# Two feed-forwards of a two-block float32 kernel: gate and up as two-by-two block products with seven multiplications, down as a second phase

## The chip, the core and the metric

The kernel runs on one core of a Trainium2 chip. The metric is device time in microseconds, from the start to the end of one execution; three executions of the kernel before gave 3000.35 us in the median (3000.02 to 3003.03). The profile is taken from one further execution. Its engines are TensorE (matrix products), VectorE, ScalarE and GpSimd (elementwise work) and SyncE, whose queue issues the DMAs.

## What is computed

Two transformer blocks of different kinds follow each other, all in float32, on 1024 tokens of width 1024. Each has two kinds of attention, an output projection, a gated feed-forward of width 2816, and a gated layer embedding ("ple"). Only the feed-forwards change:

```python
# block 1, after h = h + rmsnorm(mix, attn_post_norm[i])
u = rmsnorm(h, ffn_pre_norm[i])
gate, up = jnp.split(u @ w_gate_up[i], [D_FF], axis=-1)      # (1024, 1024) @ (1024, 2 * 2816)
y = (jax.nn.silu(gate) * up) @ w_down[i]                     # (1024, 2816) @ (2816, 1024)
h = h + rmsnorm(y, ffn_post_norm[i])
h = h + (p[i] @ ple_proj[i]) * jax.nn.sigmoid(h @ ple_gate[i])

# block 2
def conv_ffn(h, w_gate, w_up, conv_w, conv_b, w_down):       # called with rms_norm(x, ffn_norm_g[i])
    s = h.shape[1]
    g = h @ w_gate
    gp = jnp.pad(g, ((0, 0), (CONV_WIDTH - 1, 0), (0, 0)))   # CONV_WIDTH = 3, along the tokens
    conv = conv_b
    for j in range(CONV_WIDTH):
        conv = conv + gp[:, j:j + s, :] * conv_w[j]
    return (jax.nn.silu(conv) * (h @ w_up)) @ w_down
```

## The kernel before

TensorE multiplies float32 as three products of split numbers. `split` makes of a tile a high part (a cast on ScalarE to a 32-bit type that the array takes, line 135) and a low part (a subtraction, line 141, on VectorE or GpSimd). `mm3` (lines 210 to 212) issues high x high, high x low and low x high into one PSUM bank. Every matmul has 128 rows, 128 columns of weights and 512 streamed columns.

The stages follow each other in time: attention of block 1, its output projection (`out1`), feed-forward `ffn(0)` from 700 to 1428 us, `ple1`, attention of block 2, `out2` to 2162 us, `ffn(1)` to about 2880, `ple2`. In `out1` and `out2` each tile of 128 tokens gets its product with the output weights, a norm, the residual (GpSimd, line 932), another norm (`u_tok`, line 453); then `transpose_split` turns it on TensorE with eight transposes and splits it into `u[half]`, the operand of the feed-forward with features on the partitions; `half` is four token tiles.

`ffn` goes over pairs of the 22 blocks of 128 hidden features. `gu_mm(f, half)` multiplies a block of gate and of up with half of the tokens, 24 matmuls each; ScalarE applies the activation (in block 2 VectorE first convolves), VectorE multiplies gate and up, and the result is split into `act`, which stays in SBUF. After a pair's four calls, `down` multiplies both blocks of `act` with their rows of `w_down` for all eight token tiles, 96 matmuls, and adds the result to `y` from PSUM.

```python
for f0, n in CHUNKS:            # pairs of blocks
    for f, h in order:
        gu_mm(f, h)             # gate and up of one block, 512 tokens: 2 x 24 matmuls
    for i in range(NT):
        down(f0, n, i)          # 2 halves of the width x 2 blocks x 3 matmuls
```

The order of the work is the order in which the program is written; each engine takes its instructions in that order and waits for what it needs. Weights come through the class `Weights`: a list of units of 512 KB in the order of use, loaded by SP into two raw buffers and split into slots (four for kind "w", gate and up; three for kind "x", down) as `pump`, called after every step, finds a free slot.

Of the kernel before, what the change touches and what calls it, by code (L numbers as in the profile page):

```python
# [8 lines left out]
F32 = mybir.dt.float32  # L9
F32R = mybir.dt.float32r  # L10
# [36 lines left out]
CHUNKS = [(f, 2) for f in range(0, NF, 2)]  # L47


class Weights:  # L50
# [3 lines left out]
    def __init__(self, k, raws):  # L54
        self.k, self.raws = k, raws
        self.src, self.kind, self.tile, self.raw = [], [], {}, {}
# [4 lines left out]
    def open(self, kind, slots, ctx):  # L61
        self.pool[kind] = self.k.pool(kind + str(self.n_split), slots, ctx=ctx)
        self.slots[kind] = slots
        self.live[kind] = 0

    def add(self, src, kind="w"):
        self.src.append(src)
        self.kind.append(kind)
        return len(self.src) - 1

    def _dma(self):
        u = self.n_dma
        raw = self.k.rawp.tile([P, 1024], F32, tag="raw", name="raw")
        a, b = self.src[u].shape[1:]
        self.k.nc.sync.dma_start(out=raw.rearrange("p (a b) -> p a b", a=a) if b * a == 1024 else
                                 raw.rearrange("p (a b) -> p a b", a=a)[:, :, 0:b], in_=self.src[u])
        self.raw[u] = (raw, a, b)
        self.n_dma += 1

    def _split(self):  # L80
        k, u = self.k, self.n_split
        while self.n_dma <= u:
            self._dma()
        raw, a, b = self.raw.pop(u)
        kind = self.kind[u]
        w = self.pool[kind].tile([P, 2, 1024], F32R, tag=kind, name=kind)
        view = lambda t: t.rearrange("p (a b) -> p a b", a=a)[:, :, 0:b]
        k.split(view(w[:, 0, :]), view(w[:, 1, :]), view(raw), k.w_hi, k.w_lo[u % len(k.w_lo)])
# [3 lines left out]
        while self.n_dma < len(self.src) and self.n_dma - self.n_split < self.raws:  # L92
            self._dma()
# [6 lines left out]
    def pump(self, n=9):  # L100

        while n and self.n_split < len(self.src):
            kind = self.kind[self.n_split]
            if self.live[kind] >= self.slots[kind]:
                break
# [8 lines left out]
class Kernel:  # L114
# [119 lines left out]


# [29 lines left out]
    def row_units(self, name, r0, n):  # L265
        w = self.A[name][0]
        return [self.W.add(w[(r0 + j) * P:(r0 + j + 1) * P, :].rearrange("p (a n) -> p a n", a=1), "x") for j in range(n)]
# [30 lines left out]
    def ffn_units(self, s, gate, up, u0, down):  # L298
        U = self.U
        for f0, n in CHUNKS:  # L300
            for f in range(f0, f0 + n):
                U["g", s, f] = self.a_units(gate, f * P, 1)[0]
                U["u", s, f] = self.a_units(up, u0 + f * P, 1)[0]
            for f in range(f0, f0 + n):
                U["d", s, f] = self.row_units(down, f, 1)[0]
# [44 lines left out]
    def build(self):  # L350
# [4 lines left out]
        self.rawp = self.pool("raw", RAWS)  # L355
        self.W = Weights(self, RAWS)
        self.W.open("w", 4, self.ctx)
# [5 lines left out]
            rm=[4, 2, T], dv=[T, 512], omT=[512, T], od=[T, 512], bias8=[4, 1152], skew=[4, P * 1152]).items()}  # L363
# [92 lines left out]
    def block1(self):  # L456
# [9 lines left out]
        with ExitStack() as c1:  # L466
            self.up = self.pool("u_a", 2, ctx=c1)
            with ExitStack() as c2:
                yp = self.pool("y", 1, ctx=c2)
                self.y = [yp.tile([P, D], F32, tag=f"y{i}", name=f"y{i}") for i in range(NT)]  # L470
                self.W.open("x", 3, c2)
                self.out1()
                self.pre = self.pool("pre0", 1, ctx=c2)

                nc.sync.dma_start(out=S["skew"].rearrange("h (r x) -> h r x", r=P),
                                  in_=S["bias8"].unsqueeze(1).to_broadcast([4, P, 1152]))
                self.ffn(0)
                self.ple1()
            rest = self.block2_in(c1)
            self.mla(rest)  # L480
        with ExitStack() as c1:
# [1159 lines left out]
```

## Time and profile before

| | us |
|---|---|
| median of three runs | 3000.35 |
| profiled execution, whole | 3009.19 |
| profiled execution, span from first to last instruction | 3007.4 |
| TensorE busy | 2888.8 (96% of the span) |
| VectorE, ScalarE, GpSimd busy | 1559.0, 1030.8, 398.2 |
| `ffn(0)`; `ffn(1)` | from 700 to 1428; from 2162 to about 2880 |

Times from the trace are counted from the span's start. "Busy" of TensorE counts a matmul from its start to the end of its last column, and matmuls overlap; the rate is read from the distance between two starts. A bracket at the end of a timeline row gives how long the engine was idle before it and what it waited for.

### The profile page before, as it was taken

What the parts mean: (1) busy time and instruction counts of PE and PEld (TensorE: products, weight loads), DVE (VectorE), ACT (ScalarE), POOL (GpSimd) and SP (SyncE); (2) the same over time, 40 slices, a digit from 0 to 9 for tenths busy, and PEclk for the clock granted to TensorE, in tenths of its full rate; (3) what the DMA queues carried; (4) which work ended last, traced back from release to release, by engine and by line L of the source; (5) the groups of instructions that cost most, each with busy time, mean ns of one, the idle gap of its engine ahead of it and who ended that gap; (6) DMA issues with size and microseconds to landing.
All of it is one profiled execution on the core that took longest, in us unless ns stands there. A gap on an engine that the chain in (4) does not pass through costs nothing.

```text
span 3007.4 us, 36884 instructions
## 1 busy us (share of the span) xinstructions
PE 2888.8 (96%) x14227; PEld 2384.4 (79%) x14227; DVE 1559.0 (52%) x3004; ACT 1030.8 (34%) x2096; POOL 398.2 (13%) x444
## 2 busy tenths in 40 slices
PE   8989998889999999999899999989999999999999
PEld 6878776777888888888788788767888888888877
DVE  4444678754233232334568775778744444444462
ACT  4121566643211111112236455656421211122231
POOL 1223000131100010011314100010011111111111
PEclk9999999999999999999999999989999999999999
DMA  4112554334211111111135764864311111111111
GB/s 132 64 50 99 147 146 124 130 130 128 63 42 50 42 51 48 49 57 56 55 113 159 204 162 129 192 170 104 102 54 45 49 57 42 50 43 56 42 65 46
DMA packets 256622, 266.80 MB, mean 89 GB/s; under 512 B 12278, under 2 KB 204826, under 8 KB 254910
## 3 DMA queue, kind: packets, MB, share of 16 engines
q1 hardware_dynamic: 256446, 264.44, 30.1%
q8 instruction: 112, 1.84, 0.3%
q14 instruction: 64, 0.52, 0.1%
HBM read 201.43 MB, written 65.33 MB: 89 GB/s over the span
## 4 chain that ended last, share of the span: by engine, by line
PE 66%; DVE 5%; DMA 4%; ACT 1%; POOL 1%; issue 1%; SPq 0%; DVEq 0%; ACTq 0%; POOLq 0%
PE bank L212 20%; PE bank L210 20%; PE bank L211 20%; PE bank L198 1%; PE bank L1455 1%; PE bank L745 1%; DMA om_r<-rm 1%; DMA qk<-qkT 1%; DMA strip<-skew 1%; POOL y L932 1%; PE bank L758 1%; DMA o_sb<-osbT 0%; DVE qk L1207 0%; DVE y L453 0%; PE bank L1338 0%
## 5 line engine op out<-in xcount | busy, mean ns | idle before, releaser
L210 PE MATMUL bank<-u,w 128*128 128x512 f32 x1664 | 652.5, 392 | 2.3 <-DVE hq L540 1.7
L212 PE MATMUL bank<-u,w 128*128 128x512 f32 x1664 | 649.9, 391 | 0.0
L211 PE MATMUL bank<-u,w 128*128 128x512 f32 x1664 | 649.8, 390 | 0.0
L210 PEld LDWEIGHTS bank<-u,w 128*128 128x128 f32 x1664 | 312.9, 188 | 66.5 <-DVE hq L540 1.9
L212 PEld LDWEIGHTS bank<-u,w 128*128 128x128 f32 x1664 | 312.9, 188 | 64.0
L211 PEld LDWEIGHTS bank<-u,w 128*128 128x128 f32 x1664 | 312.8, 188 | 62.6
L210 PE MATMUL bank<-w,u 128*128 128x512 f32 (+1 forms) x736 | 297.8, 405 | 5.7 <-ACT w L135 3.4
L211 PE MATMUL bank<-w,u 128*128 128x512 f32 (+1 forms) x736 | 291.1, 396 | 2.2 <-POOL w L141 1.3
L212 PE MATMUL bank<-w,u 128*128 128x512 f32 (+1 forms) x736 | 292.4, 398 | 0.0
L141 DVE TENSOR_TENSOR w<-raw,w 128x1024 fp32r<-128x1024 f32 (+1 forms) x154 | 190.1, 1236 | 182.8 <-ACT w L135 182.4
L212 PE MATMUL bank<-x,act 128*128 128x512 f32 x704 | 273.9, 389 | 0.0
L210 PE MATMUL bank<-x,act 128*128 128x512 f32 x704 | 273.9, 389 | 0.0
L211 PE MATMUL bank<-x,act 128*128 128x512 f32 x704 | 273.9, 389 | 0.0
L141 POOL TENSOR_TENSOR act<-sg,act 128x512 fp32r<-128x512 f32 x88 | 136.6, 1553 | 918.3 <-ACT act L135 918.3
L994 DVE TENSOR_TENSOR sg<-sg,bank 128x512 f32<-128x512 f32 x88 | 60.5, 688 | 338.7 <-PE bank L212 336.3
L135 ACT CAST w<-raw 128x1024 fp32r<-128x1024 f32 (+1 forms) x158 | 165.1, 1046 | 138.0 <-PE bank L212 115.2
L135 ACT CAST x<-raw 128x1024 fp32r<-128x1024 f32 x53 | 55.7, 1051 | 357.2 <-PE bank L212 352.5
L210 PEld LDWEIGHTS bank<-w,u 128*128 128x128 f32 x736 | 140.2, 191 | 31.1 <-ACT u L203 4.2
L211 PEld LDWEIGHTS bank<-w,u 128*128 128x128 f32 x736 | 140.1, 190 | 27.2 <-POOL w L141 2.2
L212 PEld LDWEIGHTS bank<-w,u 128*128 128x128 f32 x736 | 140.3, 191 | 26.8 <-DVE u L206 0.2
L1012 DVE TENSOR_TENSOR yy<-yy,bank 128x512 f32<-128x512 f32 x176 | 118.6, 684 | 79.7 <-PE bank L212 79.7
L211 PEld LDWEIGHTS bank<-x,act 128*128 128x128 f32 x704 | 132.2, 188 | 27.5
(319 smaller groups left out, 4693.1 us busy)
## 6 DMA issues: line engine op xcount, KB each, us to landing
raw<-in_w_gate_up_dram SPq DMA_DIRECT2D x44, 512.0 KB
raw<-in_w_down_dram SPq DMA_DIRECT2D x44, 512.0 KB
raw<-in_w_in_dram SPq DMA_DIRECT2D x40, 512.0 KB
qk<-qkT SPq DMA_DIRECT2D x32, 384.0 KB
raw<-in_w_gate_dram SPq DMA_DIRECT2D x22, 512.0 KB
raw<-in_w_up_dram SPq DMA_DIRECT2D x22, 512.0 KB
k<-sk SPq DMA_DIRECT2D x16, 512.0 KB
raw<-in_w_out_dram SPq DMA_DIRECT2D x16, 512.0 KB
```

What stands on the lines that cost most here:

```text
L135: nc.scalar.copy(hi, src)
L141: e.tensor_tensor(lo, src, hi.bitcast(F32), ALU.subtract)
L198: nc.tensor.transpose(ps[:, j * P:(j + 1) * P], src[:, (g + j) * P:(g + j + 1) * P], self.ident)
L210: mm(ps, lh, rh, start=start, stop=False)
L211: mm(ps, lh, rl, start=False, stop=False)
L212: mm(ps, ll, rh, start=False, stop=stop)
L745: nc.tensor.transpose(ps[:, n * P:(n + 1) * P], a[:, j * P:(j + 1) * P], self.ident)
L758: nc.tensor.matmul(pv[:, 0:256], vs[:, j0, :], at[:, hl, 0:256], start=jp == 0 and hl == 0, stop=False)
L932: nc.gpsimd.tensor_tensor(y, y, x, ALU.add)
L994: nc.vector.tensor_tensor(sg, sg, pu, ALU.mult)
L1012: nc.vector.tensor_tensor(y, y, ps, ALU.add)
L1455: nc.tensor.matmul(pv[:, 0:P], at[:, n * P:(n + 1) * P], x["v"][:, j, :], start=j == 0, stop=j == i)
```

## The change

The product of the weights (a pair of blocks x 1024 features) with the tokens is taken as a two-by-two block product: the pair's two blocks are the rows, the lower and the upper 512 features the inner index, and the even and the odd token tiles the columns. It is formed with seven products of half the inner length instead of eight, from sums and differences of the four weight blocks and of the four operand blocks. A **chain** is one pair of gate or of up; there are 22 in a feed-forward. A product is 12 matmuls (4 steps of 128 features, 3 each), numbered 1 to 7. Products 1, 6, 7 and 4 go into one bank one upon the other, 5 and 3 into a second, 2 into a third, and ScalarE copies intermediate states to SBUF (`keep`), where VectorE adds them to others.

The weights of a chain are four units: the raw first block, `s12`, a difference, and a half-width one; GpSimd forms the last three with four operations on half tiles (`add_pair`). The operand blocks other than 1 and 2 are formed by `right_operands` on GpSimd and VectorE. The activated result goes to a DRAM tensor `act`, and after all chains `down` loads it back and does the 1056 matmuls that it did before. In the second feed-forward the residual also goes to DRAM (`h3`) and is loaded back as `y` ahead of `down`. Weights of `down` take slots of kind "w".

```diff
+PART = {1: (0, 0), 2: (0, 1), 6: (1, 0), 5: (1, 1), 7: (2, 0), 4: (2, 1), 3: (3, 0)}
+def sevens(s, chains):
+    if s == 0:
+        seq = [(c, p) for p in (1, 2, 6, 5, 7, 4, 3) for c in (0, 1)]
+        late = []
+    else:
+        seq = [(0, 1), (0, 2), (1, 1), (0, 6), (0, 5), (0, 7), (0, 4), (0, 3), (1, 2), (1, 6), (1, 5), (1, 7)]
+        late = [(1, 4), (1, 3)]
+    for c in range(2, chains):
+        seq += [(c, 1)] + late + [(c, 2), (c, 6), (c, 5), (c, 7)]
+        late = [(c, 4), (c, 3)]
+    return seq + late
...
+    def add_pair(self, src1, src2):
...
+        def m1(w, lo):
+            both(w, st["r1"], lo)
+        def m2(w, lo):
+            r1, r2 = st["r1"], st["r2"]
+            x = k.xp.tile([P, 1024], F32, tag="x", name="s12")
+            pool(x[:, HI], r2[:, LO], r2[:, HI], ALU.add)
+            pool(x[:, LO], x[:, HI], r1[:, LO], ALU.subtract)
+            pool(r2[:, LO], r1[:, LO], r2[:, LO], ALU.subtract)
+            pool(r1[:, HI], r1[:, HI], x[:, LO], ALU.subtract)
+            both(w, x, lo)
...
+        with ExitStack() as c1:
+            self.up = self.pool("u_b", 1, ctx=c1, side="right")
+            self.open_y(c1, 1)
+            for i in range(NT):
+                ld(out=self.y[i], in_=S["h3"][i * P:(i + 1) * P, :])
+            self.down(1)
+            self.ple2(c1)
...
-                return lambda: self.transpose_split(u, self.u[i // 4], 0, i % 4, 8)
+                return lambda: self.put_uT(u, i)
...
+    def right_operands(self, q2):
+        B11, B12, B21, B22 = (self.uT[n] for n in ((0, 0), (0, 1), (1, 0), (1, 1)))
+        T2 = self.q(q2)
+        for n, pools, value, steps in (
+                (6, (q2, q2), T2, [sub(pool, B11, B12, B11), sub(dve, T2, B22, B11)]),
+                (5, (q2, q2), B11, []),
+                (7, (q2, q2), B12, [sub(pool, B12, B22, B12)]),
+                (4, (self.q1, self.q1), B21, [sub(pool, B21, B21, T2)]),
+                (3, (q2, self.q1), B22, [])):
+            hi, lo = self.ub[n] = tuple(self.q(p, F32R) for p in pools)
+            for h in range(2):
+                c = slice(h * 256, (h + 1) * 256)
+                for f in steps:
+                    f(c)
+                self.split(hi[:, :, c], lo[:, :, c], value[:, :, c], "act", "dve")
...
+        def product(c, n):
...
+            for k in range(4):
+                nc.tensor.matmul(ps, w[:, 0, o], uh[:, k, :], start=first_mm, stop=False, skip_group_check=True)
+                nc.tensor.matmul(ps, w[:, 0, o], ul[:, k, :], start=False, stop=False, skip_group_check=True)
+                nc.tensor.matmul(ps, w[:, 1, o], uh[:, k, :], start=False, stop=k == 3, skip_group_check=True)
...
+            if n == 1:
+                keep(c, 1, ps)
+            elif n == 2:
+                ev(c, 0, 0, ps, x.pop(1))
+            elif n == 6:
+                keep(c, 2, ps)
+            elif n == 7:
+                keep(c, 3, ps)
+                ev(c, 1, 1, x["b"], x.pop(3))
+            elif n == 4:
+                ev(c, 1, 0, ps, None)
+            elif n == 3:
+                ev(c, 0, 1, ps, x.pop(2))
+            self.W.pump()
...
+            def load(f):
+                r = rp.tile([P, T], F32, tag="r", name="act_raw")
+                nc.sync.dma_start(out=r, in_=S["act"][f * P:(f + 1) * P, :])
+                a = acts[f] = actp.tile([P, 2, T], F32R, tag="act", name="act")
+                self.split(a[:, 0], a[:, 1], r, "act", "dve" if f < 2 else "gps")
...
+            for f in range(2):
+                load(f)
             for f0, n in CHUNKS:
...
                 for i in range(NT):
-                    down(f0, n, i)
+                    if i in (1, 4):
+                        load(f0 + n + i // 4)
+                    out(f0, n, i)
```

Three places show what stands in the queues. GpSimd between the residual of the last token tile and the first activated tile of `ffn(0)`, before:

```order
L932 TENSOR_TENSOR y5_5005<-y5_5005,x_res_5836 128x1024
L932 TENSOR_TENSOR y6_5006<-y6_5006,x_res_5944 128x1024
L932 TENSOR_TENSOR y7_5007<-y7_5007,x_res_6075 128x1024
L141 TENSOR_TENSOR act_6198<-sg_6199,act_6198 128x512
L141 TENSOR_TENSOR act_6254<-sg_6255,act_6254 128x512
L141 TENSOR_TENSOR act_6198<-sg_6310,act_6198 128x512
```

and after (`q` are operand blocks, `s12` and `raw` weights of a chain):

```order
L1044 TENSOR_TENSOR y_5995<-y_5995,x_res_6070 128x1024
L1101 TENSOR_TENSOR q_5006<-q_5008,q_5006 128x4x256
L1101 TENSOR_TENSOR q_5008<-q_5009,q_5008 128x4x256
L141 TENSOR_TENSOR s12_6152<-raw2_6149 128x512
L1101 TENSOR_TENSOR q_5007<-q_5007,q_6169 128x4x256
L142 TENSOR_TENSOR s12_6152<-s12_6152,raw_5172 128x512
L143 TENSOR_TENSOR raw2_6149<-raw_5172,raw2_6149 128x512
L144 TENSOR_TENSOR raw_5172<-raw_5172,s12_6152 128x512
```

Behind the last residual, where the first low part of an activation stood, are now three differences of operand blocks and the four weight operations of the first chain, one of which comes ahead of the third difference.

SP's queue at the end of gate and up of the second feed-forward, before (the last weights of down, then those of the embedding step):

```order
L75 DMA raw_22620<-in_w_down_2_dram 128x1024
L75 DMA raw_22625<-in_w_down_2_dram 128x1024
L75 DMA raw_22630<-in_w_ple_gate_2_dram 128x2x512
L75 DMA raw_22763<-in_w_ple_gate_2_dram 128x2x512
L75 DMA raw_22895<-in_w_ple_gate_2_dram 128x2x512
L75 DMA raw_22900<-in_w_ple_gate_2_dram 128x2x512
```

and after (`o` is activated output on its way to `act`, `y` the residual, `act_raw` the activations for `down`):

```order
L111 DMA raw_21878<-in_w_down_2_dram 128x1024
L592 DMA y0_21912<-h3_84 128x1024
L1181 DMA act_85<-o_21892 128x512
L111 DMA raw_21899<-in_w_down_2_dram 128x1024
L592 DMA y1_21913<-h3_84 128x1024
L592 DMA y2_21914<-h3_84 128x1024
L592 DMA y3_21915<-h3_84 128x1024
L592 DMA y4_21916<-h3_84 128x1024
L592 DMA y5_21917<-h3_84 128x1024
L592 DMA y6_21918<-h3_84 128x1024
L592 DMA y7_21919<-h3_84 128x1024
L1230 DMA act_raw_21940<-act_85 128x1024
L1230 DMA act_raw_21945<-act_85 128x1024
```

The two activation loads stand behind the store of the last output, two weight loads and all residual tiles.

ScalarE in the second feed-forward, one pair before (`g` is gate, `sg` the activated gate):

```order
L982 COPY g_22405<-bank1_22353 128x512
L993 ACTIVATE sg_22404<-cv_22410 128x512
L135 CAST act_22403<-sg_22404 128x512
L982 COPY g_22469<-bank5_22418 128x512
L135 CAST w_22480<-raw_22218 128x1024
L993 ACTIVATE sg_22468<-cv_22472 128x512
```

and after, around the same number of matmuls (`s` are the copies by `keep`, `cv` a convolved row of 1024 tokens):

```order
L219 CAST w_21501<-raw2_21374 128x1024
L219 CAST w_21524<-raw_21414 128x1024
L1167 ACTIVATE cv_21496<-cv_21496 128x1024
L219 CAST w_21544<-raw_21286 128x512
L1134 COPY s_21561<-bank1_21468 128x512
L219 CAST w_21576<-s12_21577 128x1024
L1167 ACTIVATE cv_21519<-cv_21519 128x1024
L1134 COPY s_21596<-bank1_21468 128x512
L1134 COPY s_21615<-bank0_21602 128x512
```

The second activation of `cv` now stands directly ahead of the copy of the bank that product 4 goes on to use.

## Rows read from the trace of the kernel before

**Rows 1.** The page, busy time of each engine and its share of the span
```profile
PE 2888.8 (96%) x14227; PEld 2384.4 (79%) x14227; DVE 1559.0 (52%) x3004; ACT 1030.8 (34%) x2096; POOL 398.2 (13%) x444
```

**Rows 2.** Stretches of time: start:end, length, busy us by engine, clock, DMA share, GB/s
```profile
760.00:1400.00 640.00, 640.00 (x2825) 530.11 (x2824) 195.31 (x240) 109.54 (x147) 60.11 (x39) 1.00 0.16 48
...
2162.00:2220.00 58.00, 58.00 (x264) 47.98 (x263) 33.40 (x45) 20.60 (x29) 8.57 (x11) 1.00 0.32 100
```

**Rows 3.** Timeline of TensorE, inside the first feed-forward: start us, length, instruction
```profile
899.65 0.39 PE L212 MATMUL bank<-x,act 128*128 128x512 f32 x1
...
903.96 0.39 PE L210 MATMUL bank<-x,act 128*128 128x512 f32 x1
```

**Rows 4.** Groups of instructions, 2200 to 2860: count, busy us, mean ns, idle before
```profile
L141 POOL TENSOR_TENSOR act<-sg,act 128x512 fp32r<-128x512 f32 x40 | 61.8, 1545 | 274.1 <-ACT act L135 274.1
...
L991 DVE SCALAR_TENSOR_TENSOR cv<-g,cols,cv 128x512 f32<-128x512 f32 x82 | 61.5, 750 | 2.2
...
L141 DVE TENSOR_TENSOR w<-raw,w 128x1024 fp32r<-128x1024 f32 x41 | 50.1, 1222 | 6.2 <-ACT w L135 6.2
...
L135 ACT CAST w<-raw 128x1024 fp32r<-128x1024 f32 x41 | 43.2, 1053 | 16.6 <-PE bank L212 16.6
...
L982 ACT COPY g<-bank 128x512 f32<-128x512 f32 x41 | 24.1, 589 | 175.8 <-PE bank L212 175.8
...
L989 DVE TENSOR_SCALAR cv<-g,cols 128x512 f32<-128x512 f32 x41 | 22.4, 546 | 195.0 <-ACT g L982 195.0
```

**Rows 5.** Timeline of VectorE, a low part beside work of GpSimd
```profile
952.55 1.72 DVE L141 TENSOR_TENSOR x<-raw,x 128x1024 fp32r<-128x1024 f32 x1
```

**Rows 6.** Timeline of GpSimd, alone and beside that low part
```profile
940.33 1.29 POOL L141 TENSOR_TENSOR act<-sg,act 128x512 fp32r<-128x512 f32 x1 [8.91 <-ACT act L135]
...
951.37 1.81 POOL L141 TENSOR_TENSOR act<-sg,act 128x512 fp32r<-128x512 f32 x1 [9.75 <-ACT act L135]
```

**Rows 7.** Timeline of TensorE, start of the first feed-forward
```profile
703.14 0.39 PE L211 MATMUL bank<-u,w 128*128 128x512 f32 x1
...
707.51 1.11 PE L198 MATMUL bank<-ident,u_tok 128*128 128x128 f32 x4 [3.98 <-DVE u L206]
...
720.08 1.07 PE L198 MATMUL bank<-ident,u_tok 128*128 128x128 f32 x8 [1.52 <-DVE u_tok L453]
...
720.90 0.48 PE L210 MATMUL bank<-u,w 128*128 128x512 f32 x1
```

**Rows 8.** Timeline of ScalarE, the same place
```profile
704.55 1.04 ACT L135 CAST w<-raw 128x1024 fp32r<-128x1024 f32 x1 [3.73 <-DMA raw<-in_w_gate_up_dram]
```

**Rows 9.** Timeline of GpSimd, operations on 1024 elements per partition
```profile
681.60 2.39 POOL L932 TENSOR_TENSOR y<-y,x_res 128x1024 f32<-128x1024 f32 x1 [3.78 <-DVE y L453]
...
712.97 3.31 POOL L932 TENSOR_TENSOR y<-y,x_res 128x1024 f32<-128x1024 f32 x1 [14.84 <-DVE y L453]
```

**Rows 10.** Timeline of TensorE after an idle stretch
```profile
594.69 0.63 PE L211 MATMUL bank<-w,u 128*128 128x512 f32 x1
...
597.24 0.63 PE L211 MATMUL bank<-w,u 128*128 128x512 f32 x1
```

**Rows 11.** Timeline of TensorE, start of the second feed-forward
```profile
2161.61 1.03 PE L198 MATMUL bank<-ident,u_tok 128*128 128x128 f32 x8
...
2167.37 1.06 PE L198 MATMUL bank<-ident,u_tok 128*128 128x128 f32 x8
```

**Rows 12.** Stretches of time, one weight load of 512 KB
```profile
882.00:886.00 4.00, 4.00 (x19) 3.34 (x18) 1.16 (x2) 1.56 (x3) 0.00 (x0) 1.00 0.39 131
```

**Rows 13.** Stretches of time in which the DMA engines were full
```profile
704.00:705.00 1.00, 0.00 (x0) 0.00 (x0) 0.00 (x0) 0.45 (x1) 0.00 (x0) 1.00 1.00 406
...
1900.00:1950.00 50.00, 45.50 (x279) 38.02 (x278) 36.31 (x90) 32.49 (x89) 0.00 (x0) 0.90 1.00 223
```

**Rows 14.** Timeline of TensorE, from the down projection to the embedding step
```profile
1431.72 0.50 PE L210 MATMUL bank<-x,pT 128*128 128x512 f32 x1 [2.65 <-ACT pT L203]
...
1448.80 0.69 PE L198 MATMUL bank<-ident,p_in 128*128 128x128 f32 x2 [4.94 <-DVE u L206]
```

More of the change, by code (lines that the diff above doesn't have):

```diff
@@ new lines, in _add, with _raw, load, make @@
+    def _add(self, load, make, kind):
+        self.load.append(load)
+        self.make.append(make)
+        self.kind.append(kind)
+        return len(self.kind) - 1
+    def _raw(self, where):
+        self.raw_live[where] += 1
+        return self.raw_pool[where].tile([P, 1024], F32, tag=where, name=where)
+    def add(self, src, kind="w"):
+        k, st = self.k, {}
+        a, b = src.shape[1:]
+        view = lambda t: t.rearrange("p (a b) -> p a b", a=a)[:, :, 0:b]
+        def load():
+            st["r"] = self._raw("raw")
+            k.nc.sync.dma_start(out=view(st["r"]), in_=src)
+        def make(w, lo):
+            k.split(view(w[:, 0, :]), view(w[:, 1, :]), view(st.pop("r")), k.w_hi, lo)
+            self.raw_live["raw"] -= 1
+        return self._add(("raw", load), make, kind)
@@ L80, in _split, with _loads @@
+    def _loads(self, upto):
+        while self.n_dma < min(upto, len(self.load)):
+            l = self.load[self.n_dma]
+            if l is not None:
+                if self.raw_live[l[0]] >= self.raws[l[0]]:
+                    return
+                l[1]()
+            self.n_dma += 1
     def _split(self):
         k, u = self.k, self.n_split
-        while self.n_dma <= u:
-            self._dma()
-        raw, a, b = self.raw.pop(u)
+        self._loads(u + 1)
+        assert self.n_dma > u
@@ L266, in row_units @@
         w = self.A[name][0]
-        return [self.W.add(w[(r0 + j) * P:(r0 + j + 1) * P, :].rearrange("p (a n) -> p a n", a=1), "x") for j in range(n)]
+        return [self.W.add(w[(r0 + j) * P:(r0 + j + 1) * P, :].rearrange("p (a n) -> p a n", a=1)) for j in range(n)]
     def register(self):
@@ L299, in ffn_units @@
         U = self.U
[L300 to L305, printed above, removed]
+        pairs = {}
+        for c in range(NF):
+            name, c0 = ((gate, 0), (up, u0))[c % 2]
+            w = self.A[name][0]
+            src = [w[:, c0 + (c - c % 2 + j) * P:c0 + (c - c % 2 + j + 1) * P].rearrange("(k p) n -> p k n", p=P) for j in range(2)]
+            pairs[c] = self.W.add_pair(*src)
+            U["p", s, c] = {}
+        for c, p in sevens(s, NF):
+            n = PART[p][0]
+            if n not in U["p", s, c]:
+                U["p", s, c][n] = self.W._add(*pairs[c][n], "w")
+        for f in range(NF):
+            U["d", s, f] = self.row_units(down, f, 1)[0]
     def b_steps(self, units, i_us, evac, n=512, cost=5.1):
```

297 lines of the change are left out of this document (190 added, 107 removed).

## Prediction

> **What bounds the kernel now.** First the page's busy times: TensorE is busy 96% of the span [rows 1], so a change pays only if it removes matmuls or the gaps between them. Then the busy time of each engine by stage: through the first feed-forward, and where the second one takes over from its attention block, TensorE is busy in every microsecond, at the full clock [rows 2]. Then its timeline in such a stretch: a 128x512 matmul starts every (903.96 - 899.65) / 19 = 0.2268 us [rows 3]; the 0.39 us beside each is how long one takes, not its share of the time. So inside a feed-forward time is the number of matmuls times 0.2268, and the rest is what its ends cost.
>
> **What is removed.** Gate and up of one feed-forward are 22 blocks x 2 x 2 halves x 24 = 2112 matmuls now. Afterwards they are 22 chains (a pair of blocks of gate, or of up) x 7 products x 12 = 1848; the down projection keeps its 1056. Two feed-forwards lose 2 x 264 = 528 matmuls: 528 x 0.2268 = **-119.7 us**, if TensorE stays the bound.
>
> **Does it, in the steady part?** A chain is 84 matmuls, 19.05 us; a product is 2.72 us. Per chain ScalarE makes four weight splits (3.5 tiles of 1024 columns at 1.05), three copies at 0.59 and the activations, about 8 us; VectorE the same splits' low parts (3.5 x 1.22 = 4.3) and about 3 adds, in the second feed-forward 4 us of convolution more; GpSimd four half-tile operations and some multiplications, 1.3 to 1.8 each [rows 4]: none is full. But products accumulate into one bank and ScalarE copies it between them: after product 6 the copy must be done within product 5, after product 7 within product 1 of the next chain, 2.72 us each. The queue is in order, so what stands ahead of a copy counts. The tightest place is in the second feed-forward, where ScalarE's activation of a whole convolved row stands ahead of the copy after product 7. From the end of product 4 VectorE has there: two convolutions of 1024 columns, 2 x (1.09 + 2 x 1.50) = 8.2, three low parts (1.22, 1.22, 0.61), two adds at 0.75 at most: 12.8 us, begun 0.8 us late by a copy. The activation (2 x 0.59 by the copy's row) ends at 14.8, the copy at 15.4, and it is due after six products, at 16.3. That fits by 0.9 us. What can spoil it: a low part took 1.72 us beside GpSimd's operation and GpSimd's took 1.81 beside it, 1.29 alone [rows 5, 6]. If a third of VectorE's stretch is slowed so, 12.8 grows by 1.7, a miss of 0.8; if all of it, by 5.2, a miss of 4.3. Eleven such places: 0 to 47 us. I take 0.5 each, **+5**, near the third, since GpSimd works about a third of the time. The Trainium skill (GPSIMD Engine Reference, Key points) says that GpSimd shares its SBUF interfaces with VectorE and contends with VectorE instructions that have two SBUF inputs; these rows agree, and it speaks against this change, which gives GpSimd such work in every chain.
>
> **The ends.** Before, gate and up could start on the first four token tiles while the last were normalised. Now every product streams columns of all token tiles, and only products 1 and 2 need no difference of operands. The order puts 48 matmuls ahead of the first product 6 in the first feed-forward, 36 in the second; what follows waits for GpSimd.
>
> (A) First feed-forward, in. Before, TensorE waits at 703 for tile 6 and before 720.08 for tile 7, and 48 matmuls are done at 720.90 [rows 7]. Part of that lateness was ScalarE waiting 3.73 us for a weight load [rows 8], which has long landed afterwards, so tile 7 may come up to 6 us earlier, though VectorE and ScalarE get splits of operands ahead of its norm. After tile 7's transposes come a copy (0.6), then on GpSimd two differences of 1024 elements a partition, a half-tile operation, a third difference, a half tile, then the weight's cast. The nearest rows for the wide ones are 2.39 and 3.31 [rows 9]; the half tiles 1.29 to 1.81. From the transposes' first half at 720.6: 0.6 + 3 x (2.39 to 3.31) + 2 x (1.29 to 1.55) + 1.05 = 11.4 to 14.7, so product 6 starts at 732.0 to 735.3, or 6 us earlier. Then its low part 1.22, one slow restart, and the same weight chain again for the other chain of the pair, one product behind (about 2). Against 720.90: 8 to 19 us, **+14**.
>
> A restart: after an idle stretch the matmuls started every (597.24 - 594.69) / 6 = 0.425 us [rows 10], the spacing of half the clock; some ten of them lose 2 us at most, I charge 1.
>
> (D) Second feed-forward, in. Before there is no gap [rows 2] and tile 7's transposes come at 2167.37 [rows 11]. GpSimd has four wide differences after them (9.6 to 13.2), then two half tiles (2.6 to 3.1), then the cast: from 2169.1 to 2182.3 to 2186.5. TensorE has 36 matmuls (8.2) and the transposes (1.1) from 2162.6 on. Missing: 10.4 to 14.6, a low part and a restart more: 11 to 18, **+14**.
>
> (B) First feed-forward, from gate and up to down. The activations now go through DRAM. The last stored part waits for GpSimd's multiplication, about 2.6 us after the last product (an add 0.7, a multiplication 1.3 to 1.8), and one of the two first loads back stands behind that store in SP's queue. A 512 KB load moved all its bytes within 4 us [rows 12] (131 GB/s x 4 us = 524 KB). 2.6 + 2.5 to 4 + cast 1.05 = 6 to 7.7, and a restart; 5 if the loads overlap better, 14 if the store must land first and a low part is late. **+8**.
>
> (E) Second feed-forward, the same place. SP's queue holds a weight load and seven of the eight residual tiles ahead of the two activation loads, and they can start only when the space of gate and up is free: 9 x 524 KB = 4.7 MB until the first activation has landed. In two stretches with the DMA engines full, 406 GB/s and 223 GB/s were moved [rows 13]; the first is the nearer one: weight and residual tiles of whole rows, as here. 4.7 MB / 406 = 11.6 us, / 223 = 21.2. With 2.6 before, 1 of delay, 1.05 and 1.3 for the casts: 17.5 or 27; with a restart, and up to 5 for the last activations' own wait: 15 to 33, **+20**. The Trainium skill (DMA: Bandwidth & Descriptors, Where 436 GB/s comes from) has transfers between HBM and SBUF bound by about 358 GB/s; the 406 of one microsecond is above that. By 358 the 11.6 would be 13.2.
>
> (C) From down to the layer-embedding step. Before, TensorE already waits there, 2.65 and 4.94 us [rows 14] the longest. Now its weights share four slots with down's last blocks, and the projection's load is issued behind a split that waits for them: one load (4), a cast (1.05). 24 matmuls of the gate (5.4) may go first and hide it, or not; the second embedding has the same: 0 to 10 each, **+5 twice**.
>
> **Sum.** -119.7 + 5 + 14 + 14 + 8 + 20 + 10 = -48.7, against the profiled execution's own 3009.19 us: 2960.5. That execution lies 8.84 above the median of the timed runs (3000.35), and I carry this over: **2951.7, so 2952 us**. Two runs of this kernel can be told apart from about 0.2%, 6 us.
>
> **Rivals.**
> (1) Steady stalls, slower than before. Place: the copies after products 6 and 7, 2 x 44 windows. Mechanism: an in-order queue, ScalarE's behind a cast or an activation that waits for VectorE or GpSimd. For it: the 0.9 us of slack above and the mutual slowing. Against: in the first feed-forward, without convolutions, each weight's split stands 10 us or more ahead of its use, and casts of 1.05 fit the 2.72. Price: 1 us a window is +88, less the 5 counted, so 3035; from 0.6 us a window (48.7 + 5 over 88) it is slower.
> (2) The ends are cheap: tile 7 early, GpSimd at its fast durations, embedding waits hidden, no restart: 8 + 11 + 5 + 15 = 39 and nothing steady: 3000.35 - 119.7 + 39 = 2920; 30 would make it 2911. For it: the wait that made tile 7 late [rows 8] goes, and GpSimd is quick when VectorE is idle [rows 6, 9]. Against: the orders on GpSimd and SP are fixed chains.
> (3) The ends at their upper bounds: 19 + 18 + 14 + 33 + 20 = 104 and 5 steady: 2990. For it: GpSimd beside a busy VectorE, DMA at 223 GB/s.
> (4) It doesn't do what it says: matmuls that stream the new operand tiles start further apart. Shapes and types are the same as now, so I see nothing for it; 0.24 instead of 0.2268 over 3696 matmuls would be +49: 3001.
>
> **Chances.** Forecast with its own bounds (2925 to 2982) 0.74; (2) 0.09; (3) 0.08; (1) 0.07; (4) 0.02. The range for 8 in 10 takes in most of (2) and (3): 2918 to 2992. Faster by over 0.2% (under 2994.3): 0.74 + 0.09 + 0.05 = 0.88; within: 0.05; slower: 0.07.
>
> **What would show it.** TensorE 100% busy through gate and up with 19.05 us a chain, and no idle before the matmuls of products 7 and 4; five gaps: before the first product 6 in each feed-forward (10 to 15 us, released by a ScalarE cast of the weights that waited for GpSimd), before down (6 to 8 and 16 to 27, released by ScalarE's cast of the reloaded activation), before the embedding. Wrong if gaps of about a microsecond repeat in every chain, if the gap at the second down is under 10 us, or if matmuls don't start 0.2268 apart.

## The result and the profile after

The changed kernel takes 2977.29 us (median of 4 runs, 2975.07 to 2983.0) against 3000.18 (4 runs, 2998.06 to 3003.03) for the kernel before: the ratio is 0.9926 [0.9909, 0.9943]. It is faster, as forecast, and the time lies inside the forecast's range, but the gain is 22.9 us where 48 were forecast. The profiled execution took 2983.0 us, its span is 2981.2, 26.2 below the span before.

On the page of the changed kernel (busy us of each engine, share of the span, instructions) TensorE has 528 instructions and 91.8 us of busy time less than in [rows 1], and its share fell from 96% to 94%: it now waits more.

```profile
PE 2797.0 (94%) x13699; PEld 2295.8 (77%) x13699; DVE 1757.5 (59%) x3120; ACT 1168.8 (39%) x2237; POOL 721.9 (24%) x606
```

The next view is the busy time by stretches, inside gate and up of the first and of the second feed-forward (columns as in [rows 2]: the busy time of TensorE, of its weight loads, of VectorE, ScalarE and GpSimd, then clock, DMA share and GB/s). TensorE is busy for the whole of both, at the full clock, though the others have more to do: in the first of the two VectorE is busy 40% of the time and GpSimd 38%, where [rows 2] had 31% and 9%. 1678 matmuls in 380 us is one every 0.2265 us (the count takes in one cut at the edge), against 0.2268 [rows 3].

```profile
760.00:1140.00 380.00, 380.00 (x1678) 314.67 (x1677) 151.04 (x150) 134.76 (x182) 144.80 (x109) 1.00 0.27 82
2215.00:2580.00 365.00, 365.00 (x1612) 302.24 (x1611) 202.50 (x202) 128.87 (x163) 135.35 (x118) 1.00 0.25 80
```

So the time of all 528 matmuls was gained, and the steady part costs nothing. The difference is in the ends. The timeline of TensorE in the changed kernel shows them (start, length, operation, in brackets the idle time and what ended it; L1087 transposes a token tile, L1194 to L1196 are a product's matmuls, L294 one of down; of the releasers, L219 is ScalarE's cast of a split, L1134 its copy of a bank, L1158 an add of VectorE):

```profile
722.22 0.39 PE L1196 MATMUL bank<-q,w 128*128 128x512 f32 x1
724.89 1.57 PE L1087 MATMUL bank<-ident,u_tok 128*128 128x128 f32 x8 [2.28 <-DVE u_tok L549]
...
728.40 0.55 PE L1196 MATMUL bank<-q,w 128*128 128x512 f32 x1
740.96 0.79 PE L1194 MATMUL bank<-q,w 128*128 128x512 f32 x1 [12.01 <-ACT w L219]
741.55 0.63 PE L1195 MATMUL bank<-q,w 128*128 128x512 f32 x1
...
745.39 0.58 PE L1196 MATMUL bank<-q,w 128*128 128x512 f32 x1
...
748.86 0.52 PE L1194 MATMUL bank<-q,w 128*128 128x512 f32 x1 [2.21 <-ACT w L219]
...
1162.59 0.80 PE L294 MATMUL bank<-w,act 128*128 128x512 f32 x1 [6.00 <-ACT act L219]
...
2171.06 0.79 PE L1194 MATMUL bank<-q,w 128*128 128x512 f32 x1 [11.27 <-ACT w L219]
...
2181.22 0.50 PE L1194 MATMUL bank<-q,w 128*128 128x512 f32 x1 [1.68 <-ACT s L1134]
...
2189.80 0.50 PE L1194 MATMUL bank<-q,w 128*128 128x512 f32 x1 [1.79 <-DVE gc L1158]
...
2204.58 0.50 PE L1194 MATMUL bank<-q,w 128*128 128x512 f32 x1 [1.80 <-ACT s L1134]
...
2609.72 0.79 PE L294 MATMUL bank<-w,act 128*128 128x512 f32 x1 [20.32 <-ACT act L219]
```

Tile 7's transposes come at 724.89, then six matmuls that were left, and then 12 us of idle until the first product 6 (740.96), which a ScalarE cast of the weights releases. Its matmuls start 0.427 us apart, close to the 0.425 of [rows 10]: nine intervals take the 3.84 us from 741.55 to 745.39. After the idle time the granted clock (the last figure but two) is 0.50 of full speed here, the lower of its two levels:

```profile
741.00:745.00 4.00, 4.00 (x10) 3.13 (x11) 4.00 (x3) 3.69 (x4) 3.92 (x3) 0.50 0.00 0
```

Another 2.21 us of idle follow, and a second slow stretch. The second feed-forward has the same picture, with one gap of 11.27 and three of 1.7 to 1.8 us; the downs begin after 6.00 and 20.32 us of idle.

The casts that release the two long gaps have themselves waited for GpSimd, on ScalarE's timeline:

```profile
739.86 1.04 ACT L219 CAST w<-s 128x1024 fp32r<-128x1024 f32 x1 [6.64 <-POOL s L142]
...
2169.96 1.04 ACT L219 CAST w<-s 128x1024 fp32r<-128x1024 f32 x1 [9.42 <-POOL s L142]
```

The source stands on the queue of GpSimd in the changed kernel, at the first feed-forward's start and the second's (L1101 differences of the operands, L141 to L144 weight tiles of half the width):

```profile
726.31 5.84 POOL L1101 TENSOR_TENSOR q<-q 128x1024 f32<-128x1024 f32 x2 [5.20 <-ACT q L1095]
732.11 2.24 POOL L141 TENSOR_TENSOR s<-raw 128x512 f32<-128x512 f32 x1
734.31 3.32 POOL L1101 TENSOR_TENSOR q<-q 128x1024 f32<-128x1024 f32 x1
737.59 2.24 POOL L142 TENSOR_TENSOR s<-s,raw 128x512 f32<-128x512 f32 x1
739.79 1.26 POOL L143 TENSOR_TENSOR raw<-raw,raw 128x512 f32<-128x512 f32 x1
...
2153.89 12.49 POOL L1101 TENSOR_TENSOR q<-q 128x1024 f32<-128x1024 f32 x4 [21.20 <-ACT q L1095]
```

and on VectorE beside it (L225 is the low part of a split):

```profile
730.46 8.25 DVE L225 TENSOR_TENSOR q<-q 128x1024 fp32r<-128x1024 f32 x3
...
2158.07 9.39 DVE L225 TENSOR_TENSOR q<-q 128x1024 fp32r<-128x1024 f32 x3
```

A wide difference takes 2.9 to 3.3 us (an operation of its size 2.39 in [rows 9], with VectorE idle), a half tile 2.24 (1.26 in the same list at 739.79, where VectorE is idle too), a low part 2.8 to 3.1 (1.22 [rows 4]): at this place each engine's operation is longer by nearly the length of the other's.

The next table is a ledger of the profiled spans: the us lost beyond 0.2268 for each matmul. A feed-forward is counted from the transposes of its first late token tile; these are, in the kernel before and, behind it, the changed one (the second feed-forward before is in [rows 11]):

```profile
699.96 1.04 PE L198 MATMUL bank<-ident,u_tok 128*128 128x128 f32 x8
```

```profile
704.74 1.04 PE L1087 MATMUL bank<-ident,u_tok 128*128 128x128 f32 x8
...
2146.28 1.03 PE L1087 MATMUL bank<-ident,u_tok 128*128 128x128 f32 x8
```

By that count the kernel before lost 9.8 us in its first feed-forward and 1.5 in its second, down included.

```
                                  after      before  difference  forecast
matmuls removed                                        -119.7     -119.7
steady part                       0          0           0          +5
(A) first gate and up, in        32.6        9.8       +22.8       +14
(B) first down, in                9.4        -          +9.4        +8
(D) second gate and up, in       23.8        1.5       +22.3       +14
(E) second down, in              23.8        -         +23.8       +20
stages up to (A), between the feed-forwards,
  and after the second (C is in the last two)
                4.8, 7.6 and 2.9 longer                +15.3       +10
sum                                                    -26.1      -48.7
```

### The profile page after: what moved, and what is told of

Read it like the earlier page. It is cut to its first block, busy times and chain, and to the rows that moved or that the text cites. A ratio compares the mean times of both kernels' runs of the same rounds, so it can differ in the third digit from the quotient of the medians.

```text
span 2981.2 us, 37288 instructions
## 1 busy us (share of the span) xinstructions
PE 2797.0 (94%) x13699; PEld 2295.8 (77%) x13699; DVE 1757.5 (59%) x3120; ACT 1168.8 (39%) x2237; POOL 721.9 (24%) x606
## 5 line engine op out<-in xcount | busy, mean ns | idle before, releaser
L1194 PE MATMUL bank<-q,w 128*128 128x512 f32 x1232 | 484.5, 394 | 32.3 <-ACT w L219 25.5
L1195 PE MATMUL bank<-q,w 128*128 128x512 f32 x1232 | 483.1, 392 | 0.2 <-DVE q L225 0.2
L1196 PE MATMUL bank<-q,w 128*128 128x512 f32 x1232 | 482.1, 392 | 0.0
L219 ACT CAST w<-raw 128x1024 fp32r<-128x1024 f32 (+2 forms) x246 | 236.6, 971 | 532.5 <-DVE y L1247 285.7
L225 DVE TENSOR_TENSOR w<-raw,w 128x1024 fp32r<-128x1024 f32 (+2 forms) x242 | 312.4, 1300 | 134.1 <-ACT w L219 133.3
L1247 DVE TENSOR_TENSOR y<-y,bank 128x512 f32<-128x512 f32 x336 | 227.1, 686 | 171.4 <-PE bank L296 171.3
L294 PE MATMUL bank<-w,act 128*128 128x512 f32 x704 | 276.7, 393 | 26.3 <-ACT act L219 26.3
L1194 PEld LDWEIGHTS bank<-q,w 128*128 128x128 f32 x1232 | 233.7, 190 | 85.0 <-ACT w L219 27.0
L294 PE MATMUL bank<-w,u 128*128 128x512 f32 (+1 forms) x672 | 272.9, 406 | 6.5 <-ACT u L287 3.7
L295 PE MATMUL bank<-w,act 128*128 128x512 f32 x704 | 276.2, 392 | 0.0
L296 PE MATMUL bank<-w,act 128*128 128x512 f32 x704 | 275.8, 392 | 0.1
L1195 PEld LDWEIGHTS bank<-q,w 128*128 128x128 f32 x1232 | 233.3, 189 | 49.3 <-DVE q L225 0.6
L1196 PEld LDWEIGHTS bank<-q,w 128*128 128x128 f32 x1232 | 233.2, 189 | 49.2 <-DVE w L225 0.3
L225 POOL TENSOR_TENSOR act<-act_raw,act 128x1024 fp32r<-128x1024 f32 x40 | 103.8, 2615 | 332.3 <-ACT act L219 332.3
L294 PEld LDWEIGHTS bank<-w,act 128*128 128x128 f32 x704 | 133.8, 190 | 55.0 <-ACT act L219 27.2
L1134 ACT COPY s<-bank 128x512 f32<-128x512 f32 x132 | 77.4, 588 | 200.7 <-PE bank L1196 200.7
L296 PEld LDWEIGHTS bank<-w,act 128*128 128x128 f32 x704 | 133.2, 189 | 29.2 <-DVE act L225 1.5
L295 PEld LDWEIGHTS bank<-w,act 128*128 128x128 f32 x704 | 133.6, 190 | 27.8
L294 PEld LDWEIGHTS bank<-w,u 128*128 128x128 f32 x672 | 128.0, 191 | 29.7 <-ACT u L287 4.7
L295 PEld LDWEIGHTS bank<-w,u 128*128 128x128 f32 x672 | 128.0, 190 | 25.1 <-POOL w L225 2.9
```

Of the source, the lines that this page charges most:

```text
L219: nc.scalar.copy(hi, src)
L225: e.tensor_tensor(lo, src, hi.bitcast(F32), ALU.subtract)
L294: mm(ps, lh, rh, start=start, stop=False)
L295: mm(ps, lh, rl, start=False, stop=False)
L296: mm(ps, ll, rh, start=False, stop=stop)
L1134: nc.scalar.copy(t, src)
```

## The experiments

The theory: the two gaps at the head of gate and up are GpSimd's serial work, the differences above all, made longer by VectorE working on the same memory; the gap before the second down is the queue of loads. The rival: these waits only hide another behind them (tile 7's lateness, a weight load, the slow clock), so that taking one away moves the gap and not the end. All experiments start from the changed kernel.

**The residual loads behind the first two activation loads (second down).**

```diff
-            for i in range(NT):
-                ld(out=self.y[i], in_=S["h3"][i * P:(i + 1) * P, :])
...
             for f in range(2):
                 load(f)
+            if s == 1:
+                for i in range(NT):
+                    nc.sync.dma_start(out=self.y[i], in_=S["h3"][i * P:(i + 1) * P, :])
```

> The eight residual tiles are loaded after the first two activation loads of the second down projection, not before; nothing else is changed. Theory (the gap of 20.70 us there is the queue of seven residual tiles ahead of the activations): the gap falls to 6 to 8 us, as at the first down projection (6.39), and the total by 11 to 14 us. Rival (the gap is the store of the last output and the weight loads): it falls by at most 3 us. A second rival: the residual tiles then delay the third and fourth activations, and half of the gain comes back as a gap 22 us later.

2961.56 us against 3001.73, 0.986 [0.9838, 0.9882]. The first matmul of down on TensorE's timeline of this kernel:

```profile
2589.69 0.79 PE L294 MATMUL bank<-w,act 128*128 128x512 f32 x1 [5.76 <-ACT act L219]
```

The idle is 5.76 where it was 20.32, and (E), which covers the whole of down, is 8.7 where it was 23.8: 15 us, a little more than the 11 to 14 expected, and kept to the end. In the changed kernel itself SP's queue of DMA issues reads

```profile
2593.01 4.66 SPq L592 DMA_DIRECT2D y<-h  x7
2598.38 1.61 SPq L1230 DMA_DIRECT2D act_raw<-act  x2
```

and the DMA engines are full, at 412 GB/s, for 12 us in which hardly anything else works (the stretch 2597 to 2609; the 0.37 us are ScalarE's):

```profile
2597.00:2609.00 12.00, 0.00 (x0) 0.00 (x0) 0.00 (x0) 0.37 (x1) 0.00 (x0) 0.50 1.02 412
```

So step (E) had its mechanism right. The residual tiles are needed only when a group of down is finished, and nothing became late behind the activations.

**The operand differences on VectorE instead of GpSimd.**

```diff
-        pool, dve = nc.gpsimd, nc.vector
+        pool, dve = nc.vector, nc.vector
```

> The differences of operand blocks are all taken on VectorE; GpSimd keeps only the weights. Theory (at the start of both feed-forwards GpSimd and VectorE slow each other: wide differences 2.9 to 3.3 us, half tiles 2.24, operand low parts 2.2 to 3.1 instead of 1.22): on VectorE a difference takes 1.22, low parts go back to 1.22 to 1.5, the first product 6 starts 4 to 8 us earlier in each feed-forward, total 8 to 16 us less. Rival (the starts are bound by the late weight loads and their four operations): the first product 6 moves by under 2 us, total within 4 us. A third way: the added work ahead of the last tile's norm on VectorE makes it later, total up to 5 us more.

2962.11 us, 0.986 [0.9839, 0.9881]. (A) falls from 32.6 to 23.9, (D) from 23.8 to 16.4. Of the profiled span's fall of 27.2 the two ends are 16.1; 6.1 more lie ahead of (A), in code that is the same (see below). The first product 6 on TensorE's timeline now waits 5.04 us, not 12.01, and a second wait, for a low part, follows:

```profile
718.41 1.79 PE L1087 MATMUL bank<-ident,u_tok 128*128 128x128 f32 x8 [3.60 <-DVE u_tok L549]
725.67 0.80 PE L1194 MATMUL bank<-q,w 128*128 128x512 f32 x1 [5.04 <-ACT w L219]
730.20 0.80 PE L1196 MATMUL bank<-q,w 128*128 128x512 f32 x1 [2.79 <-DVE w L225]
```

**The operand differences left out.** Of the differences only B22 - B11 is still made, on VectorE, so products 6, 7 and 4 multiply other numbers.

```diff
-                for f in steps:
+                for f in (steps if n == 6 and False else []):
                     f(c)
+                if n == 6:
+                    dve.tensor_tensor(T2[:, :, c], B22[:, :, c], B11[:, :, c], ALU.subtract)
```

> The differences that make the operands of products 6, 7 and 4 are left out, but for one on VectorE, so the output is not the reference's; loads, splits and matmuls stay. It shows what the differences cost at both starts. Theory: with GpSimd free the half tiles take 1.3 and the low parts 1.22, and the overhead of the two starts (22.8 and 22.4 us beyond the matmuls) falls by 8 to 12 each, 16 to 24 in total. Rival (late weight loads): 3 to 5 each.

One run, 2955.91 us, so the total has no interval; the ledger of its trace has (A) 23.6 and (D) 15.5, within a microsecond of the kernel that makes the differences on VectorE. So on GpSimd they cost 9.0 and 8.4 us at the two starts, and on VectorE at most one. How much of the 9.0 and 8.4 is their own length (5.84 + 3.32 and 12.49 us on GpSimd's timeline) and how much what they add to the low parts beside them, these runs don't separate. What is left of (A), 13.8 us above before, isn't theirs.

**The second feed-forward's weight tiles given their space earlier**, before the last projection of the attention, so that the first pair can be loaded and added ahead of the differences. (It wasn't tried in the first feed-forward.)

```diff
                 self.q1 = self.pool("q1b", 8, ctx=cq)
+                self.W.open_raw("raw2", 2, cq)
+                self.xp = self.pool("s12_1", 1, ctx=cq)
...
-        self.W.open_raw("raw2", 2, ctx)
-        self.xp = self.pool(f"s12_{s}", 1, ctx=ctx)
+        if s == 0:
+            self.W.open_raw("raw2", 2, ctx)
+            self.xp = self.pool(f"s12_{s}", 1, ctx=ctx)
```

> In the second feed-forward alone the second raw buffers and the tile for s12 are opened before the output projection, so that the first chain's weights can be loaded and combined while that still runs. Theory (at the second start the path is four operand differences on GpSimd and then s12): product 6 no longer waits for s12 and its cast, the gap of 11.66 us falls to 4 to 8, total 4 to 8 us less. Rival (the operand low parts on VectorE, slowed by GpSimd, are the path): the gap moves to the next products, total within 3 us.

2969.83 us, 0.9889 [0.9868, 0.9909]. (D) 16.8 instead of 23.8, (A) 32.5 as in the changed kernel: 7 us at the place that was changed. The gap of 11.27 is gone; the longest that is left behind tile 7's transposes is 3.86 us, at 2165.94, and a low part on VectorE ends it: the gap moved in part, as the rival had it, but not in whole. The prediction had left the order of weights and differences on GpSimd as given; a third of (D)'s 22 us hangs on it.

**The three together.** No new lines; the edits of the first, second and last of these.

> The three edits of the runs before together: activations loaded ahead of the residual, differences on VectorE, second raw buffers opened early in the second feed-forward. Theory (each acts at a place of its own, but the last two share the second start): second down overhead 9, first start 24, second start 12 to 16; ratio to the kernel before 0.978 to 0.983. Rival (they share more than that): 0.984 to 0.986.

2942.15 us against 2999.25, 0.981 [0.9795, 0.9824]. (A) 23.8, (D) 9.8, (E) 9.6: at these places the gains nearly add up, 36.9 us together where the three runs had 38.3 one by one. In the medians it is 35.1 below the changed kernel, for a sum of 38.4.

**The first two chains' weight sums on VectorE too** (with the differences there), so that GpSimd has nothing to do at the two starts. It shows whether VectorE's low parts are slow by themselves or because of GpSimd.

```diff
-        pool = k.nc.gpsimd.tensor_tensor
+        pool = (eng or k.nc.gpsimd).tensor_tensor
...
-            pairs[c] = self.W.add_pair(*src)
+            pairs[c] = self.W.add_pair(*src, eng=self.nc.vector if c < 2 else None)
```

> As the run with the differences on VectorE, and the four weight operations of the first two chains of each feed-forward on VectorE too, so that GpSimd does nothing at the starts. Theory (operations of GpSimd and VectorE with two inputs in SBUF exclude each other, so that both take about 2.2 us where alone they take 1.27 and 1.22): low parts at the starts take 1.22 to 1.3, a half tile 0.65 to 0.75, and the overheads of the two starts fall from 23.9 and 16.4 to 17 to 21 and 10 to 14. Rival (the two engines work side by side, and what counts is the length of VectorE's queue): eight operations more on it, overheads 2 to 5 us longer.

2953.19 us, 0.9851 [0.9834, 0.9868]; (A) 21.2, (D) 13.1, each some 3 below the kernel with the differences alone moved. Against that kernel the medians lie 8.9 apart, but the two were timed on different occasions and their ratios overlap, so the ledger carries this one. VectorE's timeline at the second start, with GpSimd idle there:

```profile
2143.73 1.22 DVE L225 TENSOR_TENSOR w<-raw,w 128x1024 fp32r<-128x1024 f32 x1
2144.86 4.62 DVE L225 TENSOR_TENSOR q<-q 128x1024 fp32r<-128x1024 f32 x4
...
2156.28 0.68 DVE L141 TENSOR_TENSOR s<-raw 128x512 f32<-128x512 f32 x1
```

and in the kernel with only the differences moved, where the weight sums are still on GpSimd, VectorE:

```profile
2142.95 2.18 DVE L225 TENSOR_TENSOR w<-s,w 128x1024 fp32r<-128x1024 f32 x1
2145.16 2.18 DVE L225 TENSOR_TENSOR w<-raw,w 128x1024 fp32r<-128x1024 f32 x1
2147.26 6.72 DVE L225 TENSOR_TENSOR q<-q 128x1024 fp32r<-128x1024 f32 x3
```

beside its GpSimd:

```profile
2139.70 2.13 POOL L142 TENSOR_TENSOR s<-s,raw 128x512 f32<-128x512 f32 x1
2141.80 2.25 POOL L143 TENSOR_TENSOR raw<-raw,raw 128x512 f32<-128x512 f32 x1
2144.01 2.25 POOL L144 TENSOR_TENSOR raw<-raw,s 128x512 f32<-128x512 f32 x1
```

The same low part takes 1.22 (or 1.15 in a row of four) with GpSimd idle and 2.2 with GpSimd busy; GpSimd's half tile 2.13 to 2.25 there and 1.26 alone. A half tile on VectorE takes 0.68.

**All of these changes together (the differences made, on VectorE), and other slots for the weights of the last two blocks of down** (the change of slots is meant for the embedding, step (C)).

```diff
-            U["d", s, f] = self.row_units(down, f, 1)[0]
+            U["d", s, f] = self.row_units(down, f, 1, "x" if f >= NF - 2 else "w")[0]
```

> All of this together, and the last pair of down's weights in slots of kind x, so that the embedding's first weights can be split earlier. Theory: second down overhead 9, starts as in the run before or a few us better, and the stretches after the two down projections 2 us shorter each (now 2.9 and 2.8 longer than before the change); ratio to the kernel before 0.973 to 0.978. Rival on the embedding (its wait is the load of the projection, not the slots): those stretches stay.

2940.31 us, 0.9802 [0.9786, 0.9818]: not to be told from the three together (0.981), and short of the 0.973 to 0.978 expected. (A) 21.3, (D) 10.4: once the second weight space is opened early, the weight sums on VectorE gain 2.5 us in (A) and nothing in (D). From the second down to the start of the last matmul it takes 121.9 us where the kernels without the new slots have 122.6 to 123.1, not the 2 us less that were expected, and the stretch between the feed-forwards isn't shorter (740.2). So the slots gain a microsecond at most, and that isn't settled by this.

**And the first two activation blocks read back early**, during the last chain of the second feed-forward, into the weight tiles' space.

```diff
+            if s == 1 and (c, n) == (NF - 1, 6):
+                for f in range(2):
+                    r = self.early[f] = self.W.raw_pool["raw2"].tile([P, T], F32, tag="raw2", name="act_raw")
+                    nc.sync.dma_start(out=r, in_=S["act"][f * P:(f + 1) * P, :])
...
-                r = rp.tile([P, T], F32, tag="r", name="act_raw")
-                nc.sync.dma_start(out=r, in_=S["act"][f * P:(f + 1) * P, :])
+                r = self.early.get(f)
+                if r is None:
...
```

> As the run before, and in the second feed-forward the first two activation tiles are loaded during the last chain into the second raw buffers, which are free by then. Theory (the gap before down is the load, 3 to 4 us, and the cast behind it): the gap of 5.9 us falls to 1.2 to 2.5, total 3 to 5 us less than the run before. Rival (the gap is the release of the space for the split activations and the cast alone): under 1 us.

2934.04 us (2929.82 to 2938.32), 0.9784 [0.9767, 0.98]: the best of all, faster than both kernels. Down begins on TensorE's timeline after 0.93 us of idle, with the clock granted in full:

```profile
2559.20 0.47 PE L294 MATMUL bank<-w,act 128*128 128x512 f32 x1 [0.93 <-DVE o L1182]
```

(E) is 3.1 in place of 9.9; (D) is 11.7, 1.3 more than in the run before.

## Why the prediction was half right

Between the sum of the forecast, -48.7, and the ledger's -26.1 lie 22.6 us: 8.8 in (A), 8.3 in (D), 3.8 in (E), 1.4 in (B), 5.3 in the stages outside, less the 5 of the steady part. That the time still fell inside the range is in part luck: (A) and (D) lie above their own upper bounds of 19 and 18, and only the unused 5 and (B) and (E), well under their upper bounds of 14 and 33, kept the sum below the range's end.

**The steady part: right.** 528 x 0.2268 came off, no gap repeats, and the 5 us charged were 0. The tightest place, the copy behind an activation in the second feed-forward, had more slack than the 0.9 us worked out. On ScalarE's timeline of the changed kernel the copy after product 7 waits for TensorE, 0.66 us behind the activation ahead of it:

```profile
2429.00 1.06 ACT L1167 ACTIVATE cv<-cv 128x1024 f32<-128x1024 f32 x1
2430.71 0.59 ACT L1134 COPY s<-bank 128x512 f32<-128x512 f32 x1 [0.66 <-PE bank L1196]
```

One reason is that the convolution works on 1024 columns at once, and VectorE does these in less than twice the time of 512:

```profile
2417.74 0.81 DVE L1164 TENSOR_SCALAR cv<-gc,cols 128x1024 f32<-128x1024 f32 x1 [4.75 <-ACT gc L1156]
2418.59 1.28 DVE L1166 SCALAR_TENSOR_TENSOR cv<-gc,cols,cv 128x1024 f32<-128x1024 f32 x1
```

0.81 and 1.28, where the prediction took 1.09 and 1.50 from the halves in [rows 4]. Rival (1) is refuted, and (4) for the feed-forwards (for the other stages see (C)).

**Steps (A) and (D): the steps that failed, by size.** The mechanism was the one named: GpSimd's serial chain, a ScalarE cast as releaser, a first gap in the forecast 10 to 15 us. Each was put at +14; they measured +22.8 and +22.3. Three terms were wrong.

First, what follows the first product 6 was priced at a low part, one restart of 1 us, and in (A) one more weight chain of about 2: some 4.2 us in (A) and 2.2 in (D). It measured 7.5 and 9.9. In (A) the first product 6 is late by 740.96 - 4.78 - 720.90 = 15.3 us against before (4.78 is how much later the whole stage began); behind it come the second gap of 2.21 and some 4 us in the two slow stretches. In (D) 12.4 us are lost by the first product 6, inside the 10.4 to 14.6 worked out, though 48 matmuls stand ahead of it on the timeline and not the 36 counted; behind it come three more gaps of 1.7 to 1.8 us, and matmuls at half the clock's rate after the long one.

Second, tile 7 did not come up to 6 us earlier. From the transposes of the first late tile to those of tile 7 it is 724.89 - 704.74 = 20.15 us, and 720.08 - 699.96 = 20.12 before [rows 7]. GpSimd's residual of tile 7 does begin 1.1 us earlier after that first tile (716.67 - 704.74 = 11.93 us; 712.97 - 699.96 = 13.01 before), but beside VectorE's low parts of the operands it takes 4.44 us where [rows 9] had 3.31, and ends no earlier:

```profile
716.67 4.44 POOL L1044 TENSOR_TENSOR y<-y,x_res 128x1024 f32<-128x1024 f32 x1 [3.51 <-DVE y L549]
```

and VectorE beside it:

```profile
716.50 2.36 DVE L225 TENSOR_TENSOR q<-q 128x1024 fp32r<-128x1024 f32 x2
```

The prediction saw these splits and still gave the early case about half the weight.

Third, the half tiles of the chain were taken at 1.29 to 1.55 us and the low parts at 1.22; they took 2.24 and 2.8 to 3.1.

As for the cause: moving the differences off GpSimd takes 8.7 and 7.4 off, leaving them out 9.0 and 8.4, moving the weight sums as well 2.7 and 3.3 more. For (D) the early weight space took off 7.1, and with the differences moved too (D) is 9.8, 8.3 above before. Of (A) some 11 to 12 us above before remain in the best kernels, with a first gap of 5 to 7 us still in it; what sets that gap wasn't separated further. So about half of (A) is shown to be GpSimd's work and its contention with VectorE, and the cause of the other half stays open.

The contention: a low part takes 1.22 us and a half tile 1.26 alone, and some 2.2 each when both queues are full, where strict turns would make 2.48. The Trainium skill (SBUF — State Buffer, Who interferes with whom) says that a VectorE instruction with two SBUF inputs contends with a GpSimd instruction that reads SBUF, over a port pair that one of them holds at a time. The rows come near that. The prediction bounded the contention by the one pair of 1.72 and 1.81 in [rows 5, 6], where the two overlapped only in part; it charged it to the steady part, which had room for it, and to the ends, where both queues were full without a break, only by the longer of two durations (3.31 and 1.55).

**(B): right**, 9.4 for 8, released by ScalarE's cast of the reloaded activation as said. **(E): right in kind**, 23.8 for 20, inside 15 to 33; the loads ran at 412 GB/s, near the 406 taken and not the 223 of the other bound [rows 13].

**(C) and what was not foreseen.** The stages outside the feed-forwards are 4.8, 7.6 and 2.9 us longer. The first two are in part no effect of the change: over the nine profiles of the changed kernel and its variants, which differ little or not at all there, the first stage ends between 698.6 and 707.5, and the stretch between the feed-forwards lasts 733.7 to 741.0; before was profiled once, at 699.96 and 733.37. The means, 703.6 and 737.7, are some 4 us above that each. One part, in the second and the third stage, is an effect of the change: matmuls that follow one another without idle time start further apart there. At the same place of the last stage 56 us hold 244 of them, and 249 before, with the clock granted in full in both (the changed kernel first):

```profile
2916.00:2972.00 56.00, 56.00 (x244) 45.45 (x243) 9.88 (x12) 7.95 (x11) 9.05 (x7) 1.00 0.13 48
```

```profile
2943.00:2999.00 56.00, 56.00 (x249) 46.37 (x248) 9.86 (x12) 7.95 (x11) 9.01 (x7) 1.00 0.14 47
```

On the mean of that stage (of the distances from 0.215 to 0.25 us) it is 0.231 us in each of the nine profiles, and 0.2274 before; between the feed-forwards 0.2317 and 0.2300. That is 1.7 us in each of the two stages, which the prediction put at nothing. The first stage has 0.2285 in both. Why the distance grows isn't shown, and what else of the 4.8, 7.6 and 2.9 is the change stays open.

Step (C)'s own wait is there at the first embedding, but TensorE sees little of it. ScalarE's cast of the projection's weights waits 6.92 us for their load, and TensorE 1.35 us for the cast, since other matmuls go first; its longest waits are 2.9 and 2.0 us, where [rows 14] had 2.65 and 4.94. On ScalarE's timeline and then TensorE's:

```profile
1419.04 1.04 ACT L219 CAST x<-raw 128x1024 fp32r<-128x1024 f32 x1 [6.92 <-DMA raw<-in_ple_proj_dram]
```

```profile
1409.01 0.50 PE L294 MATMUL bank<-w,u 128*128 128x512 f32 x1 [2.90 <-ACT u L287]
...
1420.14 0.50 PE L294 MATMUL bank<-x,pT 128*128 128x512 f32 x1 [1.35 <-ACT x L219]
...
1437.25 0.44 PE L282 MATMUL bank<-ident,p_in 128*128 128x128 f32 x2 [2.01 <-DVE u L290]
```

## What to carry over

When a change thins out the bound engine's work by adding small work on others, the steady part may hold, as here; price the first microseconds of each phase by themselves, by the queue order of each helper engine and by durations taken while both VectorE and GpSimd are busy. A wait is not over with its first release: add the further gaps and the matmuls at half rate. And look at what stands ahead of the first load in the DMA queue: eight residual tiles that nobody needed yet cost 15 us here, and reading two blocks back during the last chain took off 6 more.

## What was unexpected on the hardware

Two engines working from the same memory slowed each other almost as if they took turns: VectorE's low part went from 1.22 to 2.18 us beside GpSimd's half tiles, these from 1.26 to 2.25, and beside wide differences the low parts took 9.39 / 3 = 3.13 and the differences 12.49 / 4 = 3.12 us, somewhat under the sum of 1.22 and 2.39. On VectorE a half tile took 0.68 us against 1.26 on GpSimd alone.
